# Rotating grouped-query heads with partition-shifted elementwise products instead of a permutation matmul

## The chip, the cores and the metric

The kernel runs on one core of one Trainium2 chip. The metric is the device time of one execution in microseconds (us), and a kernel's time is the median of its runs. The engines are named as the profile names them: PE is the matrix array (TensorE) and PEld its weight loads, DVE is VectorE, ACT is ScalarE, POOL is GpSimd, and SP issues most of the DMAs. PE, DVE, ACT, POOL and SP each have a queue of their own that is worked off in order; semaphores hold an instruction back until what it reads or overwrites is ready.

## What is computed

One inference step of a two-layer trunk for 384 tokens: 128 context tokens and 256 latent tokens. Each layer mixes tokens with four parallel groups of heads (retention, a long convolution, grouped-query attention and latent attention "MLA"), all fed by one input projection, and then runs a gated feed-forward part. The change touches only the rotary embedding of the queries and the keys of grouped-query attention, for the 256 latent tokens:

```python
def apply_rope(x, cos, sin):
    x1, x2 = jnp.split(x, 2, axis=-1)
    return jnp.concatenate([x1 * cos - x2 * sin, x1 * sin + x2 * cos], axis=-1)
...
proj = h @ p['w_in']
ret_in, hy_in, gqa_in, mla_in = jnp.split(proj, ...)
...
o_gqa = window_attention(apply_rope(gq, cos_g, sin_g), apply_rope(gk, cos_g, sin_g), gv, ...)
...
q_rope = apply_rope(q_rope, cos_m, sin_m)
```

A head has 64 features, so x1 and x2 are 32 features each. There are four query heads and two key heads.

## The kernel before

**Layout.** Activations of the mixer stand feature-major: a tile of 128 partitions holds two heads of 64 features, and its columns are tokens. The 256 latent tokens are columns 130 to 385 of such a tile. The 128 partitions are then four quarters of 32: x1 and x2 of one head, x1 and x2 of the other. The rotary embedding needs, for each quarter, the neighbouring quarter of the same head.

**The products.** Each weight tile is split into two parts of lower precision: ACT rounds it (`whi`, L358) and DVE takes the remainder (`wlo`, L359). One product with a split operand is three matmuls (L383, L384, L385). A feature-major projection of one 128-feature chunk (`fmps`) is 8 steps of 3, so 24 matmuls.

**The rotary step** stands in `gqa`, L1038 to L1053, and runs for u = 2 (the keys, tile `gkf`), then u = 0 and u = 1 (two query tiles, `gfm`): three instances in each of two layers. ACT evicts the projection (L1041). PE multiplies the evicted tile by a permutation matrix that exchanges neighbouring quarters (`gsw`, L1043, into a bank of the pool "m"). DVE multiplies that bank by the sine table (`grt`, L1045). POOL multiplies the tile in place by the cosine table (L1052), which has to wait until PE has read the tile. DVE adds the two (L1053). For the keys there is also a transpose (`gkt`, L1048) with its eviction `ko` and an output DMA, and after L1053 the split of the keys for the scores (`gqk`: ACT L1057, DVE L1058 and L1059). The queries are split later (`gqs`, L1066, L1067).

**What stands around it.** `mla` prepares the latent heads. Its rows, by their names here: `tmb` normalised latents (DVE, L969); transposes `ckt`, `qlt`, `krps` on PE (L977, L983, L988), evicted as `ckvT` (ACT, L978), `qlT` (ACT, L984) and `mk` (L990, alternately DVE and ACT); the expansions `ukps` (PE, L996; evicted by ACT L997 and DVE L998), `uvps` (PE, L1002; evicted as `mv` by ACT, L1003) and `uqps` (PE, L1009; evicted as `mq` by ACT, L1010, and rotated by DVE, L1012 to L1014, three operations for each of four heads); then the scores `sc` (PE, L1020), one for each head. All banks of these names come from one small pool ("m"), so an expansion may wait until an earlier bank has been evicted.

**Order.** A block under `tc.manual_schedule` (L1414 to L1449) fixes the order on PE, DVE, ACT and SP as the generators `ml` (MLA) and `gq` (grouped-query) are stepped in turn; it ends with the last step of the fourth head's rotation and a tiny DVE copy. The first two rotary instances of a layer (keys, first queries) lie in it; other ready work (products of later projections, weight splits, `adaps`, `adat`, `vec`) is placed between its instructions. What follows (`run(ml)`, then `run(gq)`) is ordered by the scheduler, which goes by its own estimate of what is ready; the third rotary instance lies there.

```python
for u in (2, 0, 1):
    ps = fm_mm(ws.pop(0), hi, lo) if ws else fm_proj(l, u, hi, lo)
```

Of the kernel before, what the change touches and what calls it, by code (L numbers as in the profile page):

```python
# [14 lines left out]
ALU = mybir.AluOpType  # L15
# [69 lines left out]
def _consts():  # L85
    p = np.arange(128)
    c0, c, cf = {}, {}, {}
    c0["ident"] = np.eye(128)
    perm = np.zeros((128, 128))
    perm[p ^ 32, p] = 1.0  # L90
    c["perm"] = perm
    c["iup"] = np.broadcast_to(np.arange(1, 257)[None], (128, 256))
    cos, sin = _rope(256, 64)
    c["rc"] = np.tile(np.concatenate([cos, cos], 1).T, (2, 1))
    c["rs"] = np.tile(np.concatenate([-sin, sin], 1).T, (2, 1))
    cos, sin = _rope(256, 32)
    mt = np.zeros((128, 256))
    mt[64:96] = np.concatenate([cos, cos], 1).T
    mt[96:128] = np.concatenate([-sin, sin], 1).T
    c["mrope"] = mt  # L100
    kc = np.concatenate([cos, cos], 1).reshape(2, 128, 32).transpose(1, 0, 2)
    ks = np.concatenate([-sin, sin], 1).reshape(2, 128, 32).transpose(1, 0, 2)
    c["kc"] = kc.reshape(128, 64)
    c["ks"] = ks.reshape(128, 64)
    w256 = (2 * np.arange(256) + 1) * np.pi / 512
    w128 = (2 * np.arange(128) + 1) * np.pi / 256
    a = np.outer(p + 0.5, w256)
    c["fc"] = np.cos(a)
    c["fs"] = -np.sin(a)
    c["ic"] = np.cos(a).T.reshape(2, 128, 128).transpose(1, 0, 2).reshape(128, 256)  # L110
    c["is"] = np.sin(a).T.reshape(2, 128, 128).transpose(1, 0, 2).reshape(128, 256)
    a = np.outer(p, w128)
    c["pfc"] = np.cos(a)
    c["pfs"] = -np.sin(a)
    c["two"] = np.where(p[:, None] // 64 == np.arange(2)[None, :], 1.0, 0.0)
    c["pic"] = np.cos(a).T
    c["pis"] = -np.sin(a).T
    m0 = np.where(p[None, :] <= p[:, None], 0.0, -1e30)
    m1 = np.where(p[None, :] >= p[:, None], 0.0, -1e30)
    zs, ts = _zfeat(256)  # L120
    zp, tp = _zfeat(128)
    col = np.zeros((128, 16))
    col[:, 0:3] = np.stack([-tp, -ts[:128], -ts[128:]], 1)
    for b, (w, L) in enumerate(((w256[:128], 256), (w256[128:], 256), (w128, 128))):
        col[:, 3 + 3 * b] = np.cos(w / 2) / L
        col[:, 4 + 3 * b] = np.sin(w / 2) / L
        col[:, 5 + 3 * b] = -np.cos(w / 2) / L
    col[:, 12] = 127 - p
    col[:, 13] = p
    col[:, 14] = EPS  # L130
    c0["col"] = col
    a3 = np.zeros((128, 3))
    a3[64:, 0] = 1.0
    a3[:64, 2] = 1.0
    c0["addc"] = a3
    m = np.arange(256)
    a = np.outer(m + 0.5, w256)
    cf["gc"] = np.cos(a).reshape(2, 128, 256).transpose(1, 0, 2).reshape(128, 512)
    cf["gs"] = np.sin(a).reshape(2, 128, 256).transpose(1, 0, 2).reshape(128, 512)
    a = np.outer(p + 0.5, w128)  # L140
    cf["gpc"] = np.cos(a)
    cf["gps"] = np.sin(a)
    z = np.zeros((17, 384))
    z[:, 0:128] = zp.T
    z[:, 128:384] = zs.T
    return c0, c, cf, {"z": z, "mask": np.concatenate([m0, m1], 1), "lag": np.arange(384)[None, :] - 128 - p[:, None]}
# [122 lines left out]
def trunk(ctx: ExitStack, tc: tile.TileContext, A, O, offs, depth=DEPTH):  # L269
# [755 lines left out]
    def gqa(l, mx, my, mt, M, hi, lo, tma, sink, ws):  # L1025
# [12 lines left out]
        for u in (2, 0, 1):  # L1038
            ps = fm_mm(ws.pop(0), hi, lo) if ws else fm_proj(l, u, hi, lo)
            fm = kf if u == 2 else mx.tile([128, TP], F32, tag="w15", name="gfm", bufs=11)  # L1040
            S.activation(out=fm[:, 0:TP], in_=ps[:, 0:TP], func=ACTF.Copy, scale=1.0 if u == 2 else 0.125)  # L1041
            sw = bank("m", "gsw")
            T.matmul(sw[:, 0:256], cc("perm"), fm[:, 130:386], start=True, stop=True)  # L1043
            tmp = my.tile([128, 256], F32, tag="k1", name="grt", bufs=2)
            V.tensor_tensor(out=tmp, in0=sw[:, 0:256], in1=rs_, op=ALU.mult)  # L1045
            if u == 2:
                pk = bank("m", "gkt")
                T.transpose(pk[:, 0:128], fm[:, 0:128], ident)  # L1048
                ko = my.tile([128, 128], F32, tag="ko", name="ko")
                S.copy(ko, pk[:, 0:128])  # L1050
                nc.scalar.dma_start(out=O["o_k"][l].rearrange("g t d -> t g d"), in_=ko.rearrange("t (g d) -> t g d", g=2))
            G.tensor_tensor(out=fm[:, 130:386], in0=fm[:, 130:386], in1=rc, op=ALU.mult)  # L1052
            V.tensor_tensor(out=fm[:, 130:386], in0=fm[:, 130:386], in1=tmp, op=ALU.add)  # L1053
            for g in range(2):
                a, b = halfs[g], halfs[1 - g]
                if u == 2:
                    S.copy(kh[a, g], kf[a])  # L1057
                    V.tensor_copy(kh[b, g], kf[a])  # L1058
                    V.tensor_tensor(out=kl[a, g], in0=kf[a], in1=kh[a, g], op=ALU.subtract)  # L1059
            fms.append(fm)  # L1060
            yield
# [586 lines left out]
```

## Time and profile before

| | us |
|---|---|
| median of 3 runs | 1080.4 (1078.41 to 1080.73) |
| the profiled execution | 1076.9 |
| its span in the trace | 1075.1 |
| PE busy | 1048.2 (97% of the span) |
| DVE busy | 735.1 (68%) |
| ACT busy | 512.8 (48%) |
| POOL busy | 65.9 (6%) |

Times inside the trace are counted from the start of the span. The profiled execution is 1.8 us longer than its span, and 3.5 us shorter than the median of the runs. In the trace the mean granted clock of the array is 0.994 of full speed. A row of the timeline gives the start, the duration, the engine, the line, the operation, the tile written and the tiles read, and in brackets how long the engine had been idle and what released it. Successive matmuls overlap in their rows, so what a matmul takes on PE is the distance to the start of the next one.

### The profile page before, as it was taken

How to read it: one execution, taken by the hardware profiler on the slowest of the kernel's cores; microseconds unless marked ns; L12 is line 12 of the kernel's file. 1: busy time of each engine (PE TensorE's matmuls, PEld its weight loads, DVE VectorE, ACT ScalarE, POOL GpSimd, SP SyncE). 2: the span in 40 equal slices, each digit the busy share in tenths (PEclk: the TensorE clock that was granted, in tenths of full speed). 3: DMA queues.
4: the chain of work that ended last, by engine and by line, in shares of the span. 5: the costliest groups of instructions: out<-in, count | busy, mean ns of one | idle time of the engine just before them, and what ended most of it. 6: DMA issues, size and time to landing. Idle time of an engine off the chain costs nothing.

```text
span 1075.1 us, 15668 instructions
## 1 busy us (share of the span) xinstructions
PE 1048.2 (97%) x5763; PEld 894.4 (83%) x5763; DVE 735.1 (68%) x1554; ACT 512.8 (48%) x1120; POOL 65.9 (6%) x78
## 2 busy tenths in 40 slices
PE   9999999999889999999998999999999999999997
PEld 3497777768789999989986978977899999999996
DVE  6887875576789984489957677757665455445544
ACT  5765545435744433333446554553674434334333
POOL 3210001000200000000003000101020000000000
PEclk9999999999999999999999999999989999999999
DMA  9774455747557764357656522321545334343301
GB/s 345 238 273 135 154 180 216 289 134 277 179 195 246 235 197 140 121 176 234 209 154 212 196 66 73 98 65 49 207 138 177 118 118 132 127 133 119 121 18 59
DMA packets 53305, 176.05 MB, mean 164 GB/s; under 512 B 8650, under 2 KB 10570, under 8 KB 52973
## 3 DMA queue, kind: packets, MB, share of 16 engines
q1 hardware_dynamic: 49517, 171.19, 47.6%
q10 hardware_dynamic: 3712, 3.87, 1.0%
q8 instruction: 45, 0.74, 0.3%
q14 instruction: 31, 0.25, 0.1%
HBM read 169.60 MB, written 5.44 MB: 163 GB/s over the span
## 4 chain that ended last, share of the span: by engine, by line
PE 86%; DVE 8%; DMA 3%; ACT 2%; issue 1%; POOL 0%; DVEq 0%; SPq 0%; ACTq 0%; POOLq 0%
PE facc L1302 6%; PE facc L1304 6%; PE gps L383 6%; PE facc L1303 6%; PE gps L385 6%; PE gps L384 6%; PE ups L383 5%; PE ups L385 5%; PE ups L384 5%; PE fmps L383 3%; PE fmps L385 3%; PE fmps L384 3%; PE acc L1302 2%; PE acc L1303 2%; PE acc L1304 2%; PE adaps L407 2%
## 5 line engine op out<-in xcount | busy, mean ns | idle before, releaser
L359 DVE TENSOR_TENSOR wlo<-raw,whi 128x512 fp32r<-128x512 f32 (+2 forms) x388 | 254.2, 684 | 162.9 <-ACT whi L358 162.1
L358 ACT CAST whi<-raw 128x512 fp32r<-128x512 f32 (+2 forms) x388 | 221.1, 610 | 260.9 <-DMA raw<-in_wdn_dram 98.1
L1302 PE MATMUL facc<-whi,fah 128*128 128x512 f32 x264 | 105.1, 398 | 2.7 <-ACT fah L358 2.7
L1304 PE MATMUL facc<-whi,fal 128*128 128x512 f32 x264 | 104.8, 398 | 0.0
L1303 PE MATMUL facc<-wlo,fah 128*128 128x512 f32 x264 | 104.5, 396 | 0.0
L505 DVE SCALAR_TENSOR_TENSOR avc<-avr,cs,avc 128x1024 f32<-128x1024 f32 x56 | 70.2, 1280 | 0.2 <-DMA avr<-in_ada_dram 0.2
L383 PE MATMUL gps<-hTa,whi 128*128 128x386 f32 (+4 forms) x184 | 62.4, 339 | 0.2 <-DVE fc L1317 0.2
L383 PE MATMUL gps<-hTb,whi 128*128 128x386 f32 (+4 forms) x184 | 62.2, 338 | 0.0
L383 PE MATMUL ups<-hTa,whi 128*128 128x386 f32 (+4 forms) x184 | 62.2, 338 | 0.0
L383 PE MATMUL ups<-hTb,whi 128*128 128x386 f32 (+4 forms) x184 | 61.6, 335 | 0.6 <-ACT hTb L815 0.6
L384 PE MATMUL ups<-hTb,whi 128*128 128x386 f32 (+4 forms) x184 | 61.4, 334 | 0.8 <-POOL hTb L818 0.8
L385 PE MATMUL gps<-hTa,wlo 128*128 128x386 f32 (+4 forms) x184 | 62.1, 338 | 0.0
L385 PE MATMUL ups<-hTa,wlo 128*128 128x386 f32 (+4 forms) x184 | 61.9, 337 | 0.0
L384 PE MATMUL ups<-hTa,whi 128*128 128x386 f32 (+4 forms) x184 | 61.8, 336 | 0.0
L384 PE MATMUL gps<-hTa,whi 128*128 128x386 f32 (+4 forms) x184 | 61.8, 336 | 0.0
L385 PE MATMUL gps<-hTb,wlo 128*128 128x386 f32 (+4 forms) x184 | 61.7, 335 | 0.0
L384 PE MATMUL gps<-hTb,whi 128*128 128x386 f32 (+4 forms) x184 | 61.7, 335 | 0.0
L385 PE MATMUL ups<-hTb,wlo 128*128 128x386 f32 (+4 forms) x184 | 61.5, 334 | 0.0
L1302 PEld LDWEIGHTS facc<-whi,fah 128*128 128x128 f32 x264 | 49.8, 189 | 13.9 <-ACT fah L358 3.0
L1304 PEld LDWEIGHTS facc<-whi,fal 128*128 128x128 f32 x264 | 50.1, 190 | 12.0
L1303 PEld LDWEIGHTS facc<-wlo,fah 128*128 128x128 f32 x264 | 50.0, 190 | 10.1
L1318 ACT ACTIVATE fth<-fc 128x386 f32<-128x386 f32 x44 | 23.2, 528 | 58.5 <-DVE fc L1317 58.4
(392 smaller groups left out, 2392.6 us busy)
## 6 DMA issues: line engine op xcount, KB each, us to landing
raw<-in_wup_dram SPq DMA_DIRECT2D x88, 512.0 KB, 3.8
araw<-in_ada_dram SPq DMA_DIRECT2D x64, 512.0 KB, 4.5
raw<-in_wdn_dram SPq DMA_DIRECT2D x44, 512.0 KB, 3.8
avr<-in_ada_dram SPq DMA_DIRECT2D x32, 512.0 KB, 4.6
raw<-in_win_dram SPq DMA_DIRECT2D x30, 512.0 KB, 3.9
raw<-in_wout_dram SPq DMA_DIRECT2D x16, 512.0 KB, 3.7
gg<-gd SPq DMA_DIRECT2D x8, 512.0 KB
raw<-in_wta_dram SPq DMA_DIRECT2D x8, 416.0 KB, 3.4
```

The costliest lines, as they stand in the source:

```text
L358: S.copy(hi, src)
L359: (eng or V).tensor_tensor(out=lo, in0=src, in1=hi, op=ALU.subtract)
L383: T.matmul(out, ah, bh, start=start, stop=False)
L384: T.matmul(out, ah, bl, start=False, stop=False)
L385: T.matmul(out, al, bh, start=False, stop=stop)
L407: T.matmul(self.ps[32 * j:32 * j + 32, :], cs[:, k, :], rows[j // 2][:, 512 * (j % 2):512 * (j % 2) + 512], start=(k == self.k0), stop=(k ...
L505: V.scalar_tensor_tensor(out=acc[:, v, c], in0=raw, scalar=sc, in1=acc[:, v, c], op0=ALU.mult, op1=ALU.add)
L1302: T.matmul(acc[t][h], ah[:, cs_], wh_[:, hs], start=first, stop=False)
L1303: T.matmul(acc[t][h], ah[:, cs_], wl_[:, hs], start=False, stop=False)
L1304: T.matmul(acc[t][h], al[:, cs_], wh_[:, hs], start=False, stop=last)
L1318: S.activation(out=th, in_=c, func=ACTF.Tanh)
```

## The change

The permutation matrix, the matmul `gsw` and its bank are gone. In their place stand four products on quarters of 32 partitions: quarter a of `grt` is the neighbouring quarter b of the evicted tile times quarter b of the sine table. DVE does a = 0 and 2, POOL does a = 1 and 3; both operands are now in SBUF. The signs of the sine table are exchanged, since it is now indexed by the quarter that is read. POOL's in-place product with the cosine table has to wait for all four products, DVE's too, because it overwrites what they read. DVE's addition waits for POOL, as before.

```diff
     c0["ident"] = np.eye(128)
-    perm = np.zeros((128, 128))
-    perm[p ^ 32, p] = 1.0
-    c["perm"] = perm
...
-    c["rs"] = np.tile(np.concatenate([-sin, sin], 1).T, (2, 1))
+    c["rs"] = np.tile(np.concatenate([sin, -sin], 1).T, (2, 1))
...
             S.activation(out=fm[:, 0:TP], in_=ps[:, 0:TP], func=ACTF.Copy, scale=1.0 if u == 2 else 0.125)
-            sw = bank("m", "gsw")
-            T.matmul(sw[:, 0:256], cc("perm"), fm[:, 130:386], start=True, stop=True)
+
             tmp = my.tile([128, 256], F32, tag="k1", name="grt", bufs=2)
-            V.tensor_tensor(out=tmp, in0=sw[:, 0:256], in1=rs_, op=ALU.mult)
+            for j in range(4):
+                a, b = slice(32 * j, 32 * j + 32), slice(32 * (j ^ 1), 32 * (j ^ 1) + 32)
+                (V, G)[j % 2].tensor_tensor(out=tmp[a], in0=fm[b, 130:386], in1=rs_[b], op=ALU.mult)
             if u == 2:
```

The changed file is two or three lines shorter above these places, so a line there is 2 or 3 less than the same line before: the products L383 to L385 are L380 to L382, `wlo` is L356, `ukps` L993, the addition L1051, the cosine product L1050.

The order moves as well. On DVE around the keys of the second layer (`tmb` is the latents, `vec` a small copy of modulation values, `mk` the latent keys), before:

```order
L969 SCALAR_TENSOR_TENSOR tmb<-tmb,ry,lm 128x256 x3
L359 TENSOR_TENSOR wlo<-raw,whi 128x512 x2
L1045 TENSOR_TENSOR grt<-gsw,cst 128x256
L454 COPY vec_6492<-adat 128x8
L1053 TENSOR_TENSOR gkf<-gkf,grt 128x256
L454 COPY vec_6492<-adat 128x8
L1058 CAST gqk<-gkf 64x514
```

and after:

```order
L966 SCALAR_TENSOR_TENSOR tmb<-tmb,ry,lm 128x256 x3
L356 TENSOR_TENSOR wlo<-raw,whi 128x512 x2
L1043 TENSOR_TENSOR grt<-gkf,cst 32x256 x2
L451 COPY vec_6497<-adat 128x8 x4
L1051 TENSOR_TENSOR gkf<-gkf,grt 128x256
L356 TENSOR_TENSOR wlo<-raw,whi 128x512
L1056 CAST gqk<-gkf 64x514
```

One product from PSUM became two from SBUF, all four small copies stand ahead of the addition, and a weight split now stands ahead of the keys' split.

On DVE around the first queries of the second layer, before:

```order
L359 TENSOR_TENSOR wlo<-raw,whi 128x512 x4
L1045 TENSOR_TENSOR grt<-gsw,cst 128x256
L359 TENSOR_TENSOR wlo<-raw,whi 128x512
L1053 TENSOR_TENSOR gfm<-gfm,grt 128x256
L998 COPY mk<-ukps 64x512 x2
L1012 TENSOR_TENSOR mrt<-uqps,cst 32x256
```

and after:

```order
L356 TENSOR_TENSOR wlo<-raw,whi 128x512 x3
L1043 TENSOR_TENSOR grt<-gfm,cst 32x256 x2
L356 TENSOR_TENSOR wlo<-raw,whi 128x512
L1051 TENSOR_TENSOR gfm<-gfm,grt 128x256
L995 COPY mk<-ukps 64x512 x2
L1009 TENSOR_TENSOR mrt<-uqps,cst 32x256
```

The order is the same but for one weight split; the evictions of `ukps` and the rotation of the latent queries stand behind the addition in both.

On PE in the second layer, from the last product ahead of the expansions to the fourth latent score, before (30 products of `fmps` stand between `krps` and the first row):

```order
L1043 MATMUL gsw<-gfm,cst 128x256
L996 MATMUL ukps<-ckvT,mw 128x512 x2
L1002 MATMUL uvps<-mw,ckvT 128x256 x4
L1009 MATMUL uqps<-qlT,mw 128x384 x8
L1020 MATMUL sc<-mk,mq 128x384 x3
L383 MATMUL fmps<-hTa,whi 128x386
L384 MATMUL fmps<-hTa,whi 128x386
L385 MATMUL fmps<-hTa,wlo 128x386
L1020 MATMUL sc<-mk,mq 128x384
```

and after (24 products between `krps` and the first row):

```order
L993 MATMUL ukps<-ckvT,mw 128x512 x2
L999 MATMUL uvps<-mw,ckvT 128x256 x3
L380 MATMUL fmps<-hTa,whi 128x386
L999 MATMUL uvps<-mw,ckvT 128x256
L1006 MATMUL uqps<-qlT,mw 128x384 x8
L1017 MATMUL sc<-mk,mq 128x384 x3
L381 MATMUL fmps<-hTa,whi 128x386
L382 MATMUL fmps<-hTa,wlo 128x386
L380 MATMUL fmps<-hTa,whi 128x386
L1017 MATMUL sc<-mk,mq 128x384
```

Five products fewer (28 for 33) stand ahead of the fourth latent score. In the first layer 41 products stand ahead of `ukps` before and 24 after, and 44 and 38 ahead of the fourth score; one matmul of `adaps` (a part of the modulation that is computed in between) moves from behind that score to ahead of it. The third rotary's `gsw` stood directly ahead of the first grouped-query scores; its products on DVE and POOL now stand behind the first latent attention.

## Rows read from the trace of the kernel before

**Rows 1.** The page: busy time of PE, and the chain of work that ended last.

```profile
PE 1048.2 (97%) x5763; PEld 894.4 (83%) x5763; DVE 735.1 (68%) x1554; ACT 512.8 (48%) x1120; POOL 65.9 (6%) x78
...
PE 86%; DVE 8%; DMA 3%; ACT 2%; issue 1%; POOL 0%; DVEq 0%; SPq 0%; ACTq 0%; POOLq 0%
```

**Rows 2.** Busy time in three stretches: start:end, length, then busy us of each engine.

```profile
84.00:108.00 24.00, 22.84 (x102) 17.26 (x101) 19.60 (x41) 12.01 (x27) 2.45 (x2) 1.00 0.45 146
613.00:636.00 23.00, 21.45 (x95) 16.34 (x96) 19.90 (x44) 12.87 (x27) 1.45 (x2) 1.00 0.32 98
636.00:690.00 54.00, 54.00 (x359) 47.55 (x358) 39.12 (x103) 30.03 (x84) 0.64 (x1) 1.00 0.22 69
```

**Rows 3.** Timeline of PE, second layer: start, duration, operation, idle time before it.

```profile
613.45 0.70 PE L1043 MATMUL gsw<-gkf,cst 128*128 128x256 f32 x2 [0.51 <-ACT gkf L1041]
...
613.99 0.27 PE L1048 MATMUL gkt<-cst,gkf 128*128 128x128 f32 x1
...
615.32 0.42 PE L383 MATMUL fmps<-hTa,whi 128*128 128x386 f32 x1
...
619.65 0.34 PE L383 MATMUL fmps<-hTa,whi 128*128 128x386 f32 x1
...
621.65 0.70 PE L1043 MATMUL gsw<-gfm,cst 128*128 128x256 f32 x2 [0.78 <-ACT gfm L1041]
...
622.19 1.88 PE L996 MATMUL ukps<-ckvT,mw 128*128 128x512 f32 x4
...
633.73 0.88 PE L1020 MATMUL sc<-mk,mq 96*128 96x384 f32 x2 [0.31 <-issue]
```

**Rows 4.** Timeline of PE: first layer, and its third rotary instance.

```profile
94.38 0.70 PE L1043 MATMUL gsw<-gfm,cst 128*128 128x256 f32 x2 [0.80 <-ACT gfm L1041]
...
94.91 1.88 PE L996 MATMUL ukps<-ckvT,mw 128*128 128x512 f32 x4
...
106.50 0.88 PE L1020 MATMUL sc<-mk,mq 96*128 96x384 f32 x2 [0.36 <-DVE mq L1014]
...
140.25 0.70 PE L1043 MATMUL gsw<-gfm,cst 128*128 128x256 f32 x2
...
140.60 0.52 PE L1075 MATMUL sc<-gqk,gqs 128*128 128x384 f32 x1
```

**Rows 5.** POOL: the first keys in the timeline, all query products by form, small casts.

```profile
85.06 1.81 POOL L1052 TENSOR_TENSOR gkf<-gkf,cst 128x256 f32<-128x256 f32 x1 [24.30 <-PE gkt L1048]
...
L1052 POOL TENSOR_TENSOR gfm<-gfm,cst x4: 636/637/637, 95.2 to 665.5; 128x256 f32<-128x256 f32 x4
...
L724 POOL CAST hTa<-zero 128x8 fp32r<-128x8 f32 x8 | 1.8, 247 | 6.1 <-PE acc L1303 5.6 <-DVE one L318 0.5
```

**Rows 6.** Timeline of DVE: first layer, then second layer.

```profile
85.09 1.29 DVE L359 TENSOR_TENSOR wlo<-raw,whi 128x512 fp32r<-128x512 f32 x2
...
87.35 0.42 DVE L1053 TENSOR_TENSOR gkf<-gkf,grt 128x256 f32<-128x256 f32 x1
...
100.41 0.43 DVE L1012 TENSOR_TENSOR mrt<-uqps,cst 32x256 f32<-32x256 f32 x1 [1.32 <-ACT mq L1010]
...
614.46 0.42 DVE L1045 TENSOR_TENSOR grt<-gsw,cst 128x256 f32<-128x256 f32 x1
...
615.08 0.43 DVE L1053 TENSOR_TENSOR gkf<-gkf,grt 128x256 f32<-128x256 f32 x1
...
627.68 0.43 DVE L1012 TENSOR_TENSOR mrt<-uqps,cst 32x256 f32<-32x256 f32 x1 [2.27 <-ACT mq L1010]
```

**Rows 7.** Timeline of ACT: second layer, then one row of the first.

```profile
612.91 0.48 ACT L1041 ACTIVATE gkf<-fmps 128x386 f32<-128x386 f32 x1
...
615.54 0.62 ACT L1057 CAST gqk<-gkf 64x514 fp32r<-64x514 f32 x1 [0.98 <-DVE gkf L1053]
...
616.83 0.48 ACT L978 COPY ckvT<-ckt 128x384 f32<-128x384 f32 x1
...
88.83 1.26 ACT L1057 CAST gqk<-gkf 64x514 fp32r<-64x514 f32 x2
```

## The prediction

> **What bounds the kernel now.** I read the page first: PE is busy for 1048.2 of 1075.1 us, and 86% of the chain that ended last is PE [rows 1]. So time is lost only where PE waits, and work taken off PE shows in full only where PE has other work to put in its place. Then I read busy time by stretch. PE idles 1.16 us in the stretch of the first layer that holds the keys' and first queries' rotary steps, and 1.55 us in that of the second layer; the 54 us behind the latter are full [rows 2]. That full stretch gives a rule for the sum: a product that is not done by the end of a rotary stretch is still owed, and costs its whole length later. The timelines of PE show two kinds of wait: ahead of `gsw`, for ACT's eviction (0.51, 0.78, 0.80 us), and ahead of the fourth latent score, for the last step of the latent queries' rotation on DVE [rows 3, 4]. The second layer's row calls that wait "issue", the first layer's names DVE. That rotation is the chain to watch: twelve DVE operations about 0.45 us apart, which began at 627.68 after DVE had idled for 2.27 us for `uqps` [rows 6].
>
> **What is removed.** Six `gsw`. From one start to the next a `gsw` held PE for 0.54 us for the keys and for the first queries of the second layer, 0.53 for the first queries of the first layer [rows 3, 4], and 0.35 in the third instance [rows 4]; I take the other layer's for the same. That is 4 x 0.54 + 2 x 0.35 = 2.9 us of array time. The wait for ACT ahead of the keys' `gsw` isn't removed: `gkt` reads the same evicted tile and takes it over (0.51 us). The wait ahead of the queries' `gsw` goes, because `ukps`, which is next, doesn't read the queries. The smaller constant table I cost at nothing: it is loaded once, far ahead.
>
> **What is added, on DVE.** One operation of 0.42 us becomes two on 32 partitions. The latent rotation has such operations, 32x256 at 0.43 us [rows 6], as long as those on 128 partitions. So DVE has one more slot, about 0.45 us, per rotary step.
>
> **What is added, on POOL.** Three operations where there was one, one behind the other, because the cosine product waits for all four quarters. Undisturbed, the 128x256 product takes 0.64 us [rows 5]. No row shows POOL on 32 partitions. Bounds: 0.25 us, a small cast's [rows 5], and 0.64 us. I take 0.64, since DVE's rows show no gain from fewer partitions and the number of columns is the same. A POOL run is then 3 x 0.64 = 1.91 us. (The Trainium skill, GPSIMD Engine Reference, section 2.1, says that each core of that engine works on its own 16 partitions of an instruction; by that too a narrower tile isn't quicker, and no run here shows it.)
>
> **When POOL can start.** In the first layer POOL began the keys' product at 85.06 and took 1.81 us, 1.17 more than undisturbed; DVE was in two `wlo` (1.29 us from 85.09), whose two inputs both come from SBUF [rows 5, 6]. So POOL stood still until DVE's run of such operations was over. Before the change `grt` read PSUM and ended that run. Now its two operations read SBUF and lengthen it. I therefore let POOL's three start when DVE's dense run ends.
>
> **Second layer, keys.** ACT evicts the keys at 612.91 to 613.39 [rows 7]; DVE is in `tmb` and two `wlo` up to 614.46, where `grt` stood [rows 6]. The two new products end at 615.35, POOL's three at 617.26. The addition, before at 615.08 [rows 6], starts then: 2.2 us late. ACT's queue stands behind it: the casts of `gqk` at 617.7 instead of 615.54, then `ckvT`, which ended 1.77 us after their start [rows 7], so at 619.5. On PE, `gkt` comes where `gsw` was, 0.54 us early. The 24 products took 4.33 us (615.32 to 619.65) [rows 3]; they now begin at 614.78 and end at 619.1. `ukps` waits for `ckvT` 0.4 us, and the third and fourth `uvps` wait again for banks that ACT evicts late (about 0.8 and 1.3 us). ACT evicts the queries at about 623.3, once the `krps` copies, alternating between DVE and ACT, are through.
>
> **Second layer, first queries.** Three `wlo`, two `grt` and one more `wlo` keep DVE dense until about 625.75; POOL's three end at 627.66; addition (0.43) and the two `ukps` evictions (1.42 together, in the same tile order as before) follow. The latent rotation starts at about 629.5 instead of 627.68: the 2.27 us of idle time ahead of it have turned into DVE's own work, and 1.8 us are lost. The twelve operations are the same, so the fourth score comes at 635.5 instead of 633.73 [rows 3]. By then five products fewer are done (28 for 33), at 4.33/24 = 0.18 us each: 0.9 us owed. Loss 2.7 us; `gsw` is already out of this, since the times are absolute.
>
> **First layer.** The same walk: two `wlo`, two `grt` and one `wlo` keep DVE dense to about 87.8, the addition comes at 89.75 instead of 87.35 [rows 6], and ACT's casts at 90.2 instead of 88.83 [rows 7], since ACT had been held by something else until then. The rotation starts at about 101.8 instead of 100.41 [rows 6]: 1.4 us. Six products are owed (38 for 44, 1.1 us), and a matmul of `adaps`, about 0.25 us, is done earlier. Loss 2.2 us.
>
> **Third instance.** PE goes straight on to the scores: 0.35 us gained in each layer, 0.7. The longer POOL run lies behind the latent attention's work and I cost it at nothing; uncovered, it would cost 1.3 us each time (two more POOL operations).
>
> **Sum.** 2.7 + 2.2 - 0.7 = +4.2 us; rounding down for the estimated waits, +4.1. The profiled execution of 1076.9 would become 1081.0. The median of the runs is 3.5 us above that execution, so the time is 1080.4 + 4.1 = **1084.5 us**.
>
> **Rivals.**
>
> *POOL's run is shorter.* If POOL gets in between DVE's operations, or its narrow products cost 0.25 us, or overlap one another, the run in each place is some 0.63 us shorter (two products in the time of one). The two places of a layer lie on the same chain, so a layer loses 1.25 us less: 4.1 - 2.5 = +1.6, 1082.0 us. For it: no row shows POOL on 32 partitions. Against: the 1.81 us row. (The Trainium skill, GPSIMD Engine Reference, section 2.1, says that a core of POOL starts the next instruction as soon as its share of the last is finished, and quarters 1 and 3 lie in different cores' partitions; by that the two products would overlap and the time would be this one. No run here shows it.)
>
> *The cover holds and PE gains.* If the addition came no later than before, `ckvT` and the copies would be there when the 24 products end, and `ukps` would start at 619.1 instead of 622.19. Less the six products that then stood ahead of it (1.06 us) this gives 2.0 us in the second layer, by the same count 1.8 in the first, and 0.7 in the third instances: -4.5, 1075.9 us. Its place is the start of the latent rotation; it decides from the point where the queries' addition starts before about 624 instead of 627.7. For it speaks that DVE sat idle for 2.27 us there [rows 6]; against it, that three POOL operations replace one ahead of each addition. Half of it would be -2.2.
>
> *The order elsewhere.* The scheduler orders the rest of the mixer anew, and a wait may come or go far from the rotary steps. The stretches behind are full [rows 2], so I give it 2.5 us on either side. That the change doesn't do what it says is out: `gsw` is gone from PE's order.
>
> **How the numbers follow.** Within 0.2% (2.2 us) no measurement here would tell a difference. The forecast has 0.42, the shorter POOL run 0.31, the gain 0.20, the order elsewhere 0.07, half to each side. Slower takes the forecast and the bad half of the last (0.45); within 0.2% the shorter run and a little of the gain's nearer half (0.33); faster the rest (0.22). The range reaches down to two thirds of the gain, 1077.5, and up to the forecast with both third instances uncovered (2 x 1.3 us), 1087.1, and a little of the order's surprise, 1087.5. The forecast's own range is 1082.5 to 1087.1.
>
> **What would show it.** In the second layer: POOL's three rows end near 617.3 and 627.7; the additions start 2 and 4 us later than before; PE's rows show waits ahead of `ukps`, the third and fourth `uvps`; the latent rotation starts 1.8 us later; PE's idle time in the two stretches grows from 2.7 to nearly 10 us (the delays, the missing `gsw` and the owed products). If POOL's narrow products are well under 0.64 us or lie over one another, the second case is right; if the rotation starts at or before 627, the third. It would be wrong altogether if POOL weren't held up by DVE's two-input operations.

## The result and the profile after

The changed kernel is slower. Six runs of each gave a median of 1083.3 us (1080.75 to 1084.32) against 1079.3 us (1076.44 to 1080.73). These medians are 4.0 us (0.37%) apart; the ratio on record, which is used for every comparison below, puts the change at 0.52% slower, with a 95% interval of 0.28% to 0.76%. Timed again later (experiment e5) it was 0.73% slower (0.51% to 0.94%). The forecast was +4.1 us or 0.38%, 1084.5 us, with a range from 1077.5 to 1087.5. The time lies inside it, and the sign and the size are those of the forecast. The parts of the sum are not: most of the time that the changed kernel's trace loses stands in a place that the forecast put at nothing.

The page of the changed kernel answers to [rows 1]; the profiled execution took 1084.29 us, its span 1082.5:

```profile
PE 1055.0 (97%) x5751; PEld 894.2 (83%) x5751; DVE 741.6 (69%) x1560; ACT 512.4 (47%) x1120; POOL 74.8 (7%) x90
...
PE 83%; DVE 8%; DMA 3%; ACT 3%; issue 2%; POOL 1%; SPq 0%; DVEq 0%; ACTq 0%; POOLq 0%
```

PE has twelve rows fewer (six `gsw` of two passes), and yet it is busy for 6.8 us longer than in [rows 1]. That was not forecast, and the groups of PE by line show where it comes from. The group of `adaps`, the modulation's matmuls, before and then after (count, busy us, mean ns):

```profile
L407 PE MATMUL adaps<-araw,cs 128*32 128x512 f32 x256 | 33.5, 602 | 0.0
```

```profile
L404 PE MATMUL adaps<-araw,cs 128*32 128x512 f32 x256 | 40.6, 616 | 0.1
```

The same 256 rows cost 7.1 us more. Of this 5.95 us stand in the first layer ahead of the long convolution, and 0.87 us are one step ahead of the second layer, in a stretch of half the granted clock (0.50 from 582 to 584.5; see the last section):

```profile
582.76 1.93 PE L404 MATMUL adaps<-araw,cs 128*32 128x512 f32 x8
```

The 5.95 us have another reason. A step of `adaps` is four matmuls of two rows each, and each matmul takes 32 columns of the array. The timeline of PE shows a whole step before the change, and then pieces of steps after it:

```profile
113.47 1.07 PE L407 MATMUL adaps<-araw,cs 128*32 128x512 f32 x8
```

```profile
109.86 1.05 PE L404 MATMUL adaps<-araw,cs 128*32 128x512 f32 x4
...
115.94 1.05 PE L404 MATMUL adaps<-araw,cs 128*32 128x512 f32 x2
...
118.53 1.06 PE L404 MATMUL adaps<-araw,cs 128*32 128x512 f32 x6
```

Eight rows together last 1.07 us, and two rows alone as good as that (1.05). So the four matmuls of a step run side by side, and each piece of a split step costs as much as a whole one. In the new order 30 runs of `adaps` stand on PE instead of 25; six steps are in pieces, where it was one.

How late things come is best read from the eviction of the keys on ACT, which opens the rotary stretch in each layer. From there, in us later than in the kernel before (the last column counts PE's idle time up to the first product of the long convolution, which ends the stretch that the order touches):

| | first addition | second addition | latent rotation starts | long convolution starts | PE idle |
|---|---|---|---|---|---|
| first layer, forecast | +2.4 | | +1.4 | +1.85 | |
| first layer, after | +1.92 | +2.78 | +0.47 | +5.48 | +0.52 |
| second layer, forecast | +2.2 | +4.1 | +1.8 | +2.35 | |
| second layer, after | +1.83 | +3.32 | +0.84 | +1.42 | +0.92 |

(The forecast for the long convolution is the loss of the layer less 0.35 us for its third instance.) The two layers together come to 6.9 of the 7.4 us between the spans. In e5, the same kernel traced again, the second layer's long convolution comes 1.40 us late and the first layer's 4.11, with 4.9 us more `adaps` time there instead of 5.95 (two steps back to back at 191 us took 3.03 us in the first trace and 1.95 in e5). So the second layer's stretch repeats to a few hundredths of a microsecond, the first layer's, in which the modulation's loads arrive, to one or two.

The forecast also said that PE's idle time in the two stretches of [rows 2] would grow from 2.7 to nearly 10 us. In the same lengths of time, from where the stretches begin after the change, PE idles 1.81 and 3.31 us, so 5.1:

```profile
84.00:108.00 24.00, 22.19 (x90) 14.88 (x90) 21.21 (x43) 13.41 (x28) 4.59 (x6) 1.00 0.47 159
619.00:642.00 23.00, 19.69 (x81) 13.57 (x82) 21.39 (x44) 12.40 (x27) 5.57 (x6) 1.00 0.31 97
```

POOL and DVE, the keys of the first layer (the first row is from the kernel before), then the keys of the second, and then the second layer's queries (timeline: start, duration, operation, idle time before it):

```profile
83.11 2.06 DVE L969 SCALAR_TENSOR_TENSOR tmb<-tmb,ry,lm 128x128 f32<-128x128 f32 x6
...
83.24 2.83 DVE L966 SCALAR_TENSOR_TENSOR tmb<-tmb,ry,lm 128x128 f32<-128x128 f32 x6
83.93 1.46 POOL L1043 TENSOR_TENSOR grt<-gkf,cst 32x256 f32<-32x256 f32 x2 [23.16 <-ACT gkf L1038]
87.31 0.85 DVE L1043 TENSOR_TENSOR grt<-gkf,cst 32x256 f32<-32x256 f32 x2
88.28 1.09 POOL L1050 TENSOR_TENSOR gkf<-gkf,cst 128x256 f32<-128x256 f32 x1 [2.89 <-issue]
89.41 0.43 DVE L1051 TENSOR_TENSOR gkf<-gkf,grt 128x256 f32<-128x256 f32 x1 [0.54 <-POOL gkf L1050]
...
619.56 2.28 POOL L1043 TENSOR_TENSOR grt<-gkf,cst 32x256 f32<-32x256 f32 x2 [24.71 <-ACT gkf L1038]
620.60 1.52 DVE L1043 TENSOR_TENSOR grt<-gkf,cst 32x256 f32<-32x256 f32 x2
622.26 0.64 POOL L1050 TENSOR_TENSOR gkf<-gkf,cst 128x256 f32<-128x256 f32 x1 [0.42 <-POOL grt L1043]
622.93 0.43 DVE L1051 TENSOR_TENSOR gkf<-gkf,grt 128x256 f32<-128x256 f32 x1 [0.39 <-POOL gkf L1050]
...
632.88 0.43 DVE L1051 TENSOR_TENSOR gfm<-gfm,grt 128x256 f32<-128x256 f32 x1 [0.53 <-POOL gfm L1050]
634.54 0.43 DVE L1009 TENSOR_TENSOR mrt<-uqps,cst 32x256 f32<-32x256 f32 x1
```

In the second layer POOL took 2.28 us for its first two products while DVE was in `wlo`, and DVE's two products, 0.42 us each when undisturbed, took 1.52 together. In the first layer it was DVE that gave way first: its six `tmb` operations took 2.83 us, 2.06 in the kernel before. POOL's own two products were then done at 85.4, but its cosine product began only at 88.28, behind DVE's two, which stood behind two weight splits: in the first layer it is DVE's queue that set the end. The additions waited for POOL's cosine product (0.54 and 0.39 us), and the next weight split, the casts of the keys and ACT's queue stand behind them.

On PE, second layer:

```profile
629.05 0.70 PE L999 MATMUL uvps<-mw,ckvT 128*128 128x256 f32 x2 [0.99 <-ACT mk L987]
630.78 0.70 PE L999 MATMUL uvps<-mw,ckvT 128*128 128x256 f32 x2 [0.86 <-ACT mv L1000]
...
640.58 0.88 PE L1017 MATMUL sc<-mk,mq 96*128 96x384 f32 x2 [0.51 <-issue]
```

These are the waits that the forecast named for the third and fourth `uvps` (0.99 and 0.86 us; forecast 0.8 and 1.3), and, in the last row, the fourth latent score, which answers to the last row of [rows 3].

### The profile page after: what moved, and what is told of

Same layout as the page of the kernel before. It is cut to its first block, busy times and chain, and to the rows that moved or that the text cites. A ratio compares the mean times of both kernels' runs of the same rounds, so it can differ in the third digit from the quotient of the medians.

```text
span 1082.5 us, 15664 instructions
## 1 busy us (share of the span) xinstructions
PE 1055.0 (97%) x5751; PEld 894.2 (83%) x5751; DVE 741.6 (69%) x1560; ACT 512.4 (47%) x1120; POOL 74.8 (7%) x90
## 4 chain that ended last, share of the span: by engine, by line
PE 83%; DVE 8%; DMA 3%; ACT 3%; issue 2%; POOL 1%; SPq 0%; DVEq 0%; ACTq 0%; POOLq 0%
PE gps L380 6%; PE ups L380 6%; PE ups L382 6%; PE ups L381 6%; PE gps L382 6%; PE gps L381 6%; PE facc L1300 5%; PE facc L1302 5%; PE facc L1301 5%; PE fmps L380 3%; PE fmps L382 3%; PE fmps L381 3%; PE adaps L404 2%; PE acc L1300 2%; PE acc L1301 2%; PE acc L1302 2%
## 5 line engine op out<-in xcount | busy, mean ns | idle before, releaser
L356 DVE TENSOR_TENSOR wlo<-raw,whi 128x512 fp32r<-128x512 f32 (+2 forms) x388 | 254.9, 686 | 168.5 <-ACT whi L355 168.1
L380 PE MATMUL gps<-hTb,whi 128*128 128x386 f32 (+4 forms) x184 | 62.3, 339 | 0.0
L380 PE MATMUL gps<-hTa,whi 128*128 128x386 f32 (+4 forms) x184 | 62.3, 338 | 0.0
L380 PE MATMUL ups<-hTa,whi 128*128 128x386 f32 (+4 forms) x184 | 62.2, 338 | 0.0
L380 PE MATMUL ups<-hTb,whi 128*128 128x386 f32 (+4 forms) x184 | 61.7, 335 | 0.6 <-ACT hTb L812 0.6
L382 PE MATMUL gps<-hTa,wlo 128*128 128x386 f32 (+4 forms) x184 | 62.0, 337 | 0.0
L382 PE MATMUL ups<-hTa,wlo 128*128 128x386 f32 (+4 forms) x184 | 61.9, 337 | 0.0
L382 PE MATMUL gps<-hTb,wlo 128*128 128x386 f32 (+4 forms) x184 | 61.8, 336 | 0.0
L382 PE MATMUL ups<-hTb,wlo 128*128 128x386 f32 (+4 forms) x184 | 61.5, 334 | 0.0
```

The costliest lines, as they stand in the source:

```text
L356: (eng or V).tensor_tensor(out=lo, in0=src, in1=hi, op=ALU.subtract)
L380: T.matmul(out, ah, bh, start=start, stop=False)
L382: T.matmul(out, al, bh, start=False, stop=stop)
```

## Experiments

Two theories stood against each other. **A**, the forecast's: POOL's three operations and DVE's longer dense run delay additions, evictions and the latent rotation, and PE waits. **B**: the new order is to blame, by the split `adaps` steps above all. Each group of four experiments was timed on one chip beside the kernel before, so percentages are compared across the groups, not times.

### Keeping the modulation's steps whole (e1 to e4)

In all four the second pair of a step's matmuls goes first (it needs the later transfer) and the others are tied behind it, so that the scheduler doesn't split a step (a `NoSync` dependency sets the order of issue only; `man` is set inside the hand-ordered blocks):

```diff
-            for j in range(4):
-                T.matmul(self.ps[32 * j:32 * j + 32, :], cs[:, k, :], rows[j // 2][:, 512 * (j % 2):512 * (j % 2) + 512],
-                         start=(k == self.k0), stop=(k == last))
+            prev = None
+            for j in (2, 3, 0, 1):
+                with tc.high_priority() if prev is not None and not man else nullcontext():
+                    ins = T.matmul(self.ps[32 * j:32 * j + 32, :], cs[:, k, :], rows[j // 2][:, 512 * (j % 2):512 * (j % 2) + 512],
+                                   start=(k == self.k0), stop=(k == last)).ins
+                if prev is not None and not man:
+                    tc.add_manual_dep(ins, prev.name, mybir.DependencyInfo(
+                        mybir.DependencyClass.NoSync, mybir.DependencyReason.DATA), reason="group")
+                prev = ins
```

e1 is the kernel before with this edit alone, e2 the changed kernel, e3 the changed kernel with all four quarter products on DVE, and e4 with all four on DVE straight from PSUM:

```diff
-                (V, G)[j % 2].tensor_tensor(out=tmp[a], in0=fm[b, 130:386], in1=rs_[b], op=ALU.mult)
+                V.scalar_tensor_tensor(out=tmp[a], in0=ps[b, 130:386], scalar=1.0 if u == 2 else 0.125, in1=rs_[b], op0=ALU.mult, op1=ALU.mult)
```

> The kernel before, with the four matmuls of one modulation step (adaps, one for each column quarter of the array) kept together on PE; nothing else is changed in the source, the scheduler orders the rest anew. In the trace of the kernel before only one step is split (runs of 5 and 3), and it cost about the same. Both theories expect no change: within 2 us of the kernel before.

> The changed kernel with the four adaps matmuls of a step kept together. Theory A (my prediction: the longer POOL runs hold up the additions, ACT's evictions and the latent rotation): the loss stays, about 4 us slower than the kernel before. Theory B (the new order splits adaps steps; a split step costs PE about 1 us more, and the trace of after shows 5.95 us more adaps time in the first mixer and about 0.9 us ahead of the second): 6 to 7 us faster than the changed kernel's trace, so within 2 us of the kernel before, adaps time in the first mixer back to about 11.7 us.

> As e2, but all four quarter products on DVE; POOL does only the cosine product. DVE gets two more operations of 0.42 us, POOL two fewer of 0.64 to 0.69 us, so the run from the evicted tile to the addition is about as long (4 x 0.45 + 0.64 instead of 2 x 0.45 + up to 1.9). Theory A (the length of the run decides): 0 to 2 us faster than e2. Theory B: the same as e2 within 1 us as long as the steps stay whole.

> As e2, but all four quarter products on DVE straight from the projection's bank in PSUM (with the factor 0.125 of the queries in the same operation). They don't wait for ACT's eviction, don't read two SBUF operands, and POOL's cosine product, alone, waits for ACT only. Theory A: the additions come as early as before the change or earlier, so the array time of the six permutation products is gained: 2 to 4 us faster than the kernel before. Theory B alone: like e2, within 1 us.

Measured against the kernel before: e1 0.49% slower (0.25 to 0.72), e2 0.61% (0.40 to 0.82), e3 0.45% (0.25 to 0.65), e4 0.49% (0.31 to 0.67). `adaps` took 33.5 to 34.8 us in all of them, so the steps were whole. But the control e1, of which no change was expected, lost as much as the changed kernel: its first layer reaches the long convolution 9.0 us late, and PE idles 4.5 us more there. (Some 4 us of the 9.0 are no loss: 24 products and a step of `adaps` that stood behind this point stand ahead of it in e1.) Its row shows one reason for the idle time:

```profile
88.57 1.06 PE L418 MATMUL adaps<-araw,cs 128*32 128x512 f32 x8 [1.98 <-DMA araw<-in_ada_dram]
```

Tied to the later transfer, a step now stands on PE and waits for it. So the edit isn't neutral, and what it does to the first layer can't be used to judge B. The second layer can be used: it has no `adaps` in the stretch, and there e1 is on the kernel before to 0.01 us in every column of the table above. In e2, e3 and e4 the long convolution comes 1.80, 1.47 and 0.59 us late there. The first of these can't be set against the others: behind the same two waits for the third and fourth `uvps` that the changed kernel has (0.99 and 0.86 us), the granted clock of e2 fell to half from 636 to 639.5 us, which it did not in this stretch of the changed kernel, of e3 or of e4 (the clock is the third number from the end):

```profile
637.00:638.00 1.00, 1.00 (x3) 0.56 (x2) 0.47 (x2) 0.11 (x1) 0.81 (x1) 0.50 0.23 90
```

The changed kernel's own 1.42 (1.40 in e5) is the better base. Against it, moving POOL's two products to DVE wins nothing (1.47), and reading PSUM, which takes the second SBUF operand and the wait for ACT away, wins 0.8 us. That fits A as far as DVE's part goes, at a smaller price than forecast; it does not show a price of POOL's run by itself. The gain that A expected of e4 (2 to 4 us faster than the kernel before) did not come.

### The new arithmetic in the old order (e5 to e8)

e5 is the changed kernel again. In e6 every engine's order is fixed to that of the kernel before, by order-only dependencies between neighbours, from a table: `gsw` is left out, DVE's two products stand where its one stood, POOL's two directly ahead of the cosine product. e7 and e8 do the same with all four products on DVE, from SBUF and from PSUM.

```diff
+    for _e, (_a, _s) in ORD.items():
...
+        for _p, _c in zip(_o[_a:-1], _o[_a + 1:]):
...
+            tc.add_manual_dep(_seen[_e][_c], _seen[_e][_p].name, mybir.DependencyInfo(
+                mybir.DependencyClass.NoSync, mybir.DependencyReason.DATA), reason="order")
```

> The changed kernel once more, beside the three that follow, so that they can be compared on one chip: 0.5% slower than the kernel before, as measured.

> The arithmetic of the changed kernel in the order of the kernel before: on every engine each instruction stands where it stood before, with gsw left out, DVE's two quarter products at the place of its one, and POOL's two directly ahead of the cosine product. Theory A (the longer POOL runs hold up additions, evictions and the latent rotation): the rotation still starts 1.8 us late in the second and 1.4 us in the first layer, no products are owed now, the third instances gain 0.7: +2.5 us against the kernel before. Theory B (the loss is that of the new order, split adaps steps above all): the array time of the six permutation products and the queries' waits come free, -1 to -3.5 us against the kernel before, and adaps time in the first mixer is 11.7 us as before.

> As e6, but all four quarter products on DVE; POOL does the cosine product alone, as before the change. Theory A (POOL's run): the run from the evicted tile to the addition is 4 x 0.45 + 0.64 = 2.4 us behind DVE's dense work instead of 2 x 0.45 + 1.9 = 2.8: 0 to 1 us faster than e6. Theory B: the same as e6 within 1 us.

> As e7, but DVE's four products read the projection's bank in PSUM, so that they neither wait for ACT nor hold POOL back, and POOL's cosine product waits for ACT alone. In the third instance they stand earlier on DVE (ahead of the first eviction of transposed probabilities), since they hold the bank of the projection. Theory A: the additions come within about 1 us of their old places, PE reaches the expansions 1 to 2 us earlier in each layer: -2 to -4 us against the kernel before, and at least 3 us faster than e6. Theory B: the same as e6 within 1 us.

Measured: e5 0.73% slower than the kernel before (0.51 to 0.94), e6 0.75% (0.48 to 1.02), e7 0.92% (0.68 to 1.17), e8 0.65% (0.39 to 0.91). With no instruction moved and no step split, the change costs as much as in its own order: B is not needed for the loss, and the gain that B expected of e6 (-1 to -3.5 us) isn't there. The fixed order by itself isn't the reason: e12 below fixes the order of the kernel before in the same way, changes only the third instance, and is as fast as far as can be told. But A's number for e6 is wrong as well: +2.5 us was expected, and 0.75% are 8.1 us. The timeline of e6 shows the chain of A in one place, the first queries of the first layer:

```profile
97.08 1.58 POOL L1045 TENSOR_TENSOR grt<-gfm,cst 32x256 f32<-32x256 f32 x2 [7.03 <-ACT gfm L1040]
...
98.74 0.64 POOL L1052 TENSOR_TENSOR gfm<-gfm,cst 128x256 f32<-128x256 f32 x1
...
99.41 0.43 DVE L1053 TENSOR_TENSOR gfm<-gfm,grt 128x256 f32<-128x256 f32 x1 [1.25 <-POOL gfm L1052]
99.76 0.69 DVE L997 COPY mk<-ukps 64x512 f32<-64x512 f32 x1
...
100.50 0.70 PE L1001 MATMUL uvps<-mw,ckvT 128*128 128x256 f32 x2 [2.47 <-DVE mk L997]
```

POOL's two products (1.58 us), then its cosine product (0.64); DVE's addition, idle 1.25 us for it; the eviction of `ukps` behind the addition; and PE, 2.47 us idle, because the fourth `uvps` needs that bank. In the second layer it is a weight split on DVE, behind the same work, that PE waits for:

```profile
627.17 0.44 PE L384 MATMUL fmps<-hTa,wlo 128*128 128x386 f32 x1 [1.53 <-DVE wlo L358]
```

From the keys' eviction, e6 reaches the long convolution 4.88 us late in the first layer and 1.92 in the second. About 1.7 of the 4.88 are lost to the granted clock, which fell to half behind a wait of 1.84 us at 180 (last section). e7 was not faster than e6, as A expected, but, if anything, slower (the intervals overlap): its DVE has two operations more per step and POOL two fewer. It comes 4.53 and 4.66 us late, with a fall of the clock in each layer. So DVE's time is dear too, not POOL's alone. e8 was 1.3 us (first layer, 3.62 late, with one fall of the clock as in e6) and 0.7 us (second, 1.18) faster than e6 in these stretches, not the 3 us expected; in the third instance, where I had placed its products early, PE then waited 1.38 us for a bank that they held.

### Taking single parts away (e9 to e12)

e9 is the changed kernel in its own order, but the pieces of each split step stand together at the place of the last one. e10 and e11 are e6 without POOL's and without DVE's quarter products; they leave the rotation incomplete and serve for their times alone. In e12 only the third instance takes the new form, placed early:

```diff
             for j in range(4):
...
-                (V, G)[j % 2].tensor_tensor(out=tmp[a], in0=fm[b, 130:386], in1=rs_[b], op=ALU.mult)
+                if j % 2 == 0:
+                    V.tensor_tensor(out=tmp[a], in0=fm[b, 130:386], in1=rs_[b], op=ALU.mult)
...
-            V.tensor_tensor(out=fm[:, 130:386], in0=fm[:, 130:386], in1=tmp, op=ALU.add)
+            V.tensor_tensor(out=fm[:, 130:386], in0=fm[:, 130:386], in1=rs_, op=ALU.add)
```

That is e10; e11 keeps the odd quarters, on POOL. e12 against the kernel before, whose sine table has the other signs, so that the third instance subtracts:

```diff
+            if u == 1:
+                for j in range(4):
+                    a, b = slice(32 * j, 32 * j + 32), slice(32 * (j ^ 1), 32 * (j ^ 1) + 32)
+                    (V, G)[j % 2].tensor_tensor(out=tmp[a], in0=fm[b, 130:386], in1=rs_[b], op=ALU.mult)
+            else:
+                sw = bank("m", "gsw")
+                T.matmul(sw[:, 0:256], cc("perm"), fm[:, 130:386], start=True, stop=True)
+                V.tensor_tensor(out=tmp, in0=sw[:, 0:256], in1=rs_, op=ALU.mult)
```

> The changed kernel in its own order on every engine, but the six adaps steps that this order splits are put together again at the place of their last matmul on PE (26 runs of adaps instead of 30). Theory B (the split steps are the loss): adaps time in the first mixer falls from 17.6 to about 11.7 us and the kernel comes within 2 us of the kernel before. Theory A (the additions come late, PE waits, and a split step only fills a part of it): at most 3 us faster than the changed kernel, so 2 us or more slower than the kernel before.

> As e6 (new arithmetic in the old order), without POOL's two quarter products; the addition adds the sine table instead of grt, with the same waits. POOL does one operation per step, as before the change; DVE does one more than before. Theory A1 (POOL's run of three is the price): the additions come about 1.3 us earlier, 2 to 4 us faster than e6. Theory A2 (DVE's added operation is the price): the same as e6 within 1 us.

> As e6, without DVE's two quarter products; the addition adds the sine table instead of grt. POOL does three operations per step; DVE does one fewer than before. Theory A1: POOL starts 0.9 us earlier, because DVE's dense run is shorter by its two products, but its run is still three operations: 0 to 2 us faster than e6. Theory A2: 2 us or more faster than e6.

> The kernel before in its own order; only the third rotary instance of each layer takes the quarter products, with DVE's two and the addition placed early, among the first latent attention's transposes, where neither engine is dense. Keys and first queries keep the permutation product. The theory of the prediction: 0.35 us of array time gained in each layer and nothing in its way, -0.7 us against the kernel before, within what can be told from no change. If POOL's two operations more get in DVE's way there too: 1 to 2 us slower.

**e9** was 1.22% slower than the kernel before (0.93 to 1.51), so 5 to 7.5 us slower than the changed kernel (by its 0.73% and its 0.52%). `adaps` fell to 33.7 us, but PE idled 6.7 us more than in the kernel before up to the long convolution of the first layer, nearly half of it here:

```profile
101.97 1.00 PE L1001 MATMUL uvps<-mw,ckvT 128*128 128x256 f32 x2 [3.20 <-ACT mk L989]
```

The granted clock fell to half behind this wait and once before it, at 88.5; the two falls make 3.4 of the 8.3 us that this layer is late. Theory B in its simple form fell: the 5 us of split steps are not 5 us that can be had back, even without the clock's part. A caveat stays. Making a step whole at the place of its last piece also holds its weights' buffers longer, and the loads behind them come later; how much of the 3.2 us is that was not tried.

**e10** was 0.59% slower than the kernel before (0.35 to 0.83) and **e11** 0.55% (0.34 to 0.76), each less than e6, but by no more than the intervals allow. The stretches say more. Up to the long convolution e6 was 4.88 and 1.92 us late (first, second layer), e10 1.71 and 1.21, e11 -0.06 and 3.38. Without the falls of the clock (about 1.7 us each, in e6's first layer and in e11's second) these would be, as an estimate, 3.2 and 1.9, 1.7 and 1.2, and 0 and 1.7. The wait for the fourth `uvps` in the first layer, 2.47 us in e6, became

```profile
100.18 0.70 PE L1001 MATMUL uvps<-mw,ckvT 128*128 128x256 f32 x2 [1.94 <-DVE mk L997]
```

without POOL's products, and

```profile
101.08 0.70 PE L1001 MATMUL uvps<-mw,ckvT 128*128 128x256 f32 x2 [0.59 <-DVE mk L997]
```

without DVE's. So each half of the added work delays the eviction, and DVE's half, 0.9 us of operations, more than POOL's in this place. The expectations' A1 (POOL's run is the price) and A2 (DVE's added operation is) are both right in part. In e11's second layer a wait of 2.46 us appeared at the same `uvps`, which I can't explain from the parts left out; the fall of the clock stands behind it.

**e12** had a median of 1080.1 us against 1077.9 and a ratio of 0.08% slower (0.16% faster to 0.31% slower): no change that can be told, as expected. The expected 0.35 us for each layer can't be seen: the second layer's long convolution comes 0.01 us late. In the first layer it came 4.43 us late in the profiled execution, of which 2.53 are a wait for an eviction of transposed probabilities at 162 and about 1.7 the fall of the clock behind it. The runs as a whole don't show that loss, and why the wait came I leave open.

## Why the prediction was right, step by step

- **The sign and the size.** Right: +4.1 us was forecast, +4.0 measured between the medians of six, 5.6 and 7.9 us by the two ratios (0.52% and 0.73%). e6 shows that the new arithmetic alone, with no change of order, makes the kernel at least this much slower.
- **POOL's price on 32 partitions.** Right. In the third instance of the first layer no DVE operation on two tiles runs beside POOL's two products:

```profile
112.45 1.35 POOL L1043 TENSOR_TENSOR grt<-gfm,cst 32x256 f32<-32x256 f32 x2 [13.73 <-ACT gfm L1038]
```

  Two of them take 1.35 us, 0.68 each, against 0.64 us for 128 partitions [rows 5]. They follow one another. So the rival of a shorter run falls in two of its three forms, the cheap narrow product and the overlap; the third, that POOL gets in between DVE's operations, is the next point. With the overlap falls the rule of the Trainium skill (GPSIMD Engine Reference, section 2.1) that a core starts the next instruction when its share of the last is done, as far as it was to give an overlap here. The sentence of the same section on the 16 partitions of a core agrees with these rows.
- **POOL standing still until DVE's dense run is over.** Half right. It did in the second layer (2.28 us for two products). In the first it got in, and DVE's `tmb` grew from 2.06 to 2.83 us. The two engines hold each other up in both directions, and the forecast charged only POOL. There POOL had two of its three operations behind it when DVE's dense run ended, not none.
- **The additions.** Forecast 2.4 and 2.2 us late for the keys, measured 1.92 and 1.83; forecast 4.1 for the second layer's queries, measured 3.32. Since POOL got some of its work in between DVE's, the run ended earlier than a strict "after" would give.
- **The latent rotation.** Oversized: 1.4 and 1.8 us were forecast, 0.47 and 0.84 measured. The queries' addition came 0.8 us earlier than forecast, and the rotation follows it.
- **PE's waits and the owed products.** Right in the second layer: 0.99 and 0.86 us ahead of the third and fourth `uvps`; no wait ahead of `ukps`, where 0.4 was forecast. Oversized was the idle time as a whole, 5.1 us in the two stretches for nearly 10. The layer lost 1.42 us to the long convolution; 0.84 us of delay and 0.9 us of owed products, less 0.35 for the third instance, are 1.39. Forecast was 2.35, and the whole difference is the rotation's.
- **The third instance.** Forecast -0.7 us; e12, which has this part alone, could not tell it from nothing.
- **The order elsewhere.** Missed as a term of the forecast. It stood as a rival of 2.5 us on either side, "far from the rotary steps". In the first layer the scheduler's new order cut six `adaps` steps into pieces, 5.95 us more array time up to the long convolution, and the layer lost 5.48 us instead of 1.85. The rows nearly add up: 5.95, and 0.52 more idle time, less 1.41 for three `gsw`, are 5.1. The diff's order rows had shown one such piece (a matmul of `adaps` moved), which the forecast booked as a gain of 0.25 us; alone it held PE for about 1 us. On the other hand PE idled only 0.5 us more there, against 4.0 in e6: the new order filled waits with pieces. What the kernel would gain without the pieces is open, since e9 moved other things too.
- **The gain rival** (cover holds, -4.5 us). It fell with e6: the array time is gone there, every filler stands where it stood, and PE waits instead. The queries' addition comes 3.7 us late in the second layer, and the rival needed it within about 0.5 us of its old place.

So the number was met partly by luck, because errors offset. The rotary terms were too large, by 0.9 us in the second layer (1.42 for 2.35); in the first the rotation came 0.5 us late instead of 1.4, and most of its 5.48 us went with split steps, not with the forecast's waits. The mechanism was right in kind: it shows in the second layer's rows and in e6, e10 and e11.

## What to carry to other kernels

An operation on the array that looks like a waste (a permutation product, 0.35 to 0.54 us) can be the cheap place for it when PE has fillers and the elementwise engines are dense around it: moving it added 0.45 us to DVE and 1.3 us to POOL per step, just ahead of evictions for which PE waits. Two operands in SBUF on DVE and work on POOL at the same time are not two engines' worth of work. When a scheduler orders the code, look in the order after for operations that only pay in company, here four matmuls on a quarter of the columns each, before costing the edit itself. And before two traces are compared, look for falls of the granted clock in each: here one is worth as much as the differences that the experiments were to tell.

## What the hardware showed beyond the forecast

**Four quarter-width matmuls side by side.** A 128x32 product over 512 columns takes 1.05 us alone and 1.07 us in a step of four, as shown above; two steps back to back (16 rows) take 1.92, and a step with one product of the next (10 rows) takes as good as that, 1.90.

**A wait on PE can be paid twice.** In e7 PE waited 3.4 us for an eviction, and the granted clock fell behind the wait. Stretches of 2 us (busy time of PE, PEld, DVE, ACT, POOL, then the clock):

```profile
98.00:100.00 2.00, 1.36 (x7) 0.76 (x5) 0.94 (x3) 1.42 (x3) 0.00 (x0) 1.00 0.66 227
100.00:102.00 2.00, 0.00 (x0) 0.00 (x0) 1.16 (x4) 1.01 (x3) 0.64 (x1) 1.00 0.09 35
102.00:104.00 2.00, 1.23 (x3) 1.05 (x4) 2.00 (x5) 1.41 (x5) 0.00 (x0) 0.59 0.00 0
104.00:106.00 2.00, 2.00 (x4) 1.03 (x4) 0.52 (x1) 0.37 (x1) 0.00 (x0) 0.55 0.21 51
106.00:108.00 2.00, 2.00 (x7) 1.14 (x6) 1.12 (x3) 0.92 (x2) 0.00 (x0) 1.00 0.78 305
```

PE did nothing from 100 to 102; from 102 to 106 the granted clock was 0.59 and 0.55, so mostly at the lower of its levels (1.2 of 2.4 GHz), and then 1.00 again. That is 1.7 us of full clock lost ((0.41 + 0.45) x 2), all but some 0.2 us of it with PE at work. A drop also stands behind waits of 1.84 us (e6, at 180), 2.46 us (e11, at 630) and 2.53 us (e12, at 162), behind the two waits of 0.99 and 0.86 us close together in e2 (at 634 and 636), and in the kernel before behind waits of 2.71 us at 300 and 1.97 us at 784 (a drop of twice that cost). It doesn't come each time: the wait at the layer's border, about 2.0 us, is followed by it in the trace of after and not in that of before, and a wait of 2.77 us in e11 (at 304) is followed by none. The runs of one kernel differ with it: of the 31 runs of the kernel before beside e1, the fastest (1074.1 us) had a mean clock of 0.999 and the slowest (1082.4) one of 0.989. The variants here, whose PE waits longer, have lower mean clocks over their runs (0.989 to 0.993 in e1 to e11, 0.994 to 0.995 before). As an estimate, 0.002 of 1080 us is about 2 us, so some 2 of the 8 us by which e5 and e6 are slower go with the clock.
